# A two-layer hybrid encoder on one core: the modulation products on four 32-column tiles of TensorE, moved from the projections into the attention, and projection weights fetched three ahead

## The chip, the cores and the metric

One Trainium2 chip, of which the kernel uses one core. A core has five engines that run in parallel, each in the order of its own instruction stream: TensorE (PE, with its weight loads shown as PEld), VectorE (DVE), ScalarE (ACT), GpSimd (POOL) and SyncE (SP), which only issues DMAs here. The metric is the device time of one execution in microseconds (us).

## What is computed

The reference runs 1024 tokens of width 1024 through two layers. Each sub-layer is RMSNorm, a modulation `h * (1 + scale) + shift`, the sub-layer itself, and a gated residual add. Six vectors per layer (shift1, scale1, gate1, shift2, scale2, gate2) come from one condition vector:

```python
cond = jax.nn.silu(c)
shift1, scale1, gate1, shift2, scale2, gate2 = jnp.split(cond @ ada_w[i] + ada_b[i], 6, axis=-1)
h = modulate(rmsnorm(x, norm_mix_w[i]), shift1, scale1)
y = even_mixer(h, ...)      # layer 0: S5 state space | stick-breaking attention, one input projection
x = x + gate1[:, None, :] * y
h = modulate(rmsnorm(x, norm_ffn_w[i]), shift2, scale2)
x = x + gate2[:, None, :] * hierarchical_moe(h, ...)
```

So each of the 12 vectors ("names" below) is a product of a vector of 1024 with a 1024x1024 float32 matrix of 4 MiB. Layer 1 has other mixers; the change does not touch them.

## The kernel before

Everything that the change touches lies in layer 0, in `even` (L1979), ahead of the mixture of experts. Its work runs in these stages:

- **Prologue.** `norm_S` (L189) normalizes and transposes the tokens. The first 512 tokens are kept unmodulated until scale1 and shift1 of layer 0 are there (L2024), then `modulate` (L217) makes them, split into a high and a low part (`hTh`, `hTl`, by `split`, L136).
- **Projections.** Eight weights of 1 MiB (`wl`, L2040) are split by ACT and DVE into `wh` and `wl` (`wsplit`, L228), and TensorE multiplies them with the tokens by three matmuls for each product (`mm3`, L237): 768 matmuls of 128x512 in all. Weights come through `wload` (L74) into buffers of a ring (`ring`, L61); there are two rings of two 1 MiB buffers, and `pick` chooses one: ring 0 for the projection weights, one weight ahead, ring 1 for the modulation matrices.
- **S5 and attention.** Four S5 groups (`s5_quad`, L462) and eight query tiles of stick-breaking attention (`stick`, L283) are written in turn (L2087), and share DVE. A stick goes by key blocks: scores (L297, tile `ps_b`), two sigmoids on ACT (`keep`, `sw`), a mask on POOL, a scan on DVE (L313, tile `sP`), a product on POOL (L315), transposes (L106, `ps_a`), an eviction on ACT (L322), and the products with v (L326, `ps_d`), 288 of them in all. S5 uses the PSUM tag `e` (two banks), which the modulation products share.
- **GLU**, with the last sticks beside it (`glu`, tiles `gyh`, `gwh`), and the modulation of layer 1's shift2 and gate2.
- **Output rows.** `out_rows` makes two token tiles in float32 (L681), then the rest by `mm3` (first L240 of `ps_e<-wh,yh`).

The modulation products are made by `ada` (L142). For a name it loads four blocks of 1 MiB, each 128 partitions x 8 x 256. Most blocks go to DVE: one multiplication and seven multiply-adds of 128x256 (L160, L167) into `adacc`, whose 128 partitions TensorE then adds with a vector of ones (L179). One block of scale1 goes to TensorE directly (L177). Ten names are made before the GLU: scale1 and shift1 in the prologue, the other eight beside the projections, spread by the table `(0, 1, 1, 2, 2, 2, 0, 0)`.

The code is recorded in the order of the program, and a scheduler then sets the order of each engine's stream; so the place of an instruction is read below from the built program's order. A float32 matmul stands as two records in the trace (L326 has 288 matmuls in the code and 576 records); a transpose stands as one.

Of the kernel before, what the change touches and what calls it, by code (L numbers as in the profile page):

```python
# [9 lines left out]
FT = mybir.dt.float32  # L10
FR = mybir.dt.float32r
BF = mybir.dt.bfloat16
I32 = mybir.dt.int32
# [23 lines left out]
class Core:  # L37
# [42 lines left out]
    def consts(self):  # L80
        nc, c = self.nc, self.const
        ji = c.tile([128, 128], I32, name="ji")
        nc.gpsimd.iota(ji, pattern=[[1, 128]], base=0, channel_multiplier=-1)
        self.ident = c.tile([128, 128], FT, name="ident")
        nc.vector.tensor_scalar(self.ident, ji, 0.0, None, op0=OP.is_equal)
        self.ustrict = c.tile([128, 128], BF, name="ustrict")
        nc.vector.tensor_scalar(self.ustrict, ji, 0.0, None, op0=OP.is_gt)
        self.ones_b = c.tile([128, 128], BF, name="ones_b")
# [12 lines left out]
        nc.scalar.activation(self.cs, cr, AF.Silu)  # L101
        self.mod_d = self.dram.tile([2, 6, D], FT, name="mod_d")
# [39 lines left out]
    def ada(self, i, names, pool, tag, on_pe=((),), pool_eng=False):  # L142
# [4 lines left out]
        for m, nm in enumerate(names):  # L147
# [5 lines left out]
            for h in range(4):  # L153
                w = self.wload(aw[i, :, j * D + h * 256:j * D + (h + 1) * 256], 8)
                if h in on_pe[m % len(on_pe)]:
                    parts.append(w)
                    continue
                acc = pool.tile([128, 256], FT, name="adacc", bufs=4)
                eng = nc.gpsimd if pool_eng else nc.vector
                eng.tensor_scalar(acc, w[:, 0, :], self.cs[:, 0:1], None, op0=OP.mult)  # L160
                for k in range(1, KD):
                    wk, ck = w[:, k, :], self.cs[:, k:k + 1]
                    if pool_eng:
                        eng.tensor_scalar(wk, wk, ck, None, op0=OP.mult)
                        eng.tensor_tensor(acc, acc, wk, op=OP.add)
                    else:
# [4 lines left out]
            for h, x in enumerate(parts):  # L171
                for q in range(2):
                    qs = slice(q * 128, (q + 1) * 128)
                    p = pc[:, 2 * h + q:2 * h + q + 1]
                    if h in on_pe[m % len(on_pe)]:
# [1803 lines left out]
    def even(self, x_src):  # L1979
# [9 lines left out]
        with self.banks("pse", b=4, a=1, d=1, e=2):  # L1989
# [16 lines left out]
            with tc.tile_pool(name="hT", bufs=1, side="right") as hp, tc.tile_pool(name="wsp", bufs=1, side="right") as wp:  # L2006
# [178 lines left out]
```

## Time and profile before

| | us |
|---|---|
| median of 3 runs | 3071.89 (3069.78 to 3077.01) |
| profiled execution | 3069.93 |
| its span, first to last instruction | 3068.1 |
| of it, until the first projection matmul | 60.4 |
| projections | 223.8 |
| last projection matmul to the first sigmoid of the attention | 22.9 |
| S5 and attention, until the GLU | 240.9 |
| GLU | 92.6 |
| until the output rows by `mm3` | 57.9 |
| the rest: output rows, experts, layer 1 | 2369.6 |

Busy times are sums over one engine; a busy share is an average over stages with different limits. "Idle before" an instruction is time in which its engine stood, with what ended it. The granted clock of TensorE is given as a share of full speed; it has two levels, 2.4 and 1.2 GHz, so 0.94 over a stretch means that 12% of it ran at half speed.

### The profile page before, as it was taken

The numbers are of one execution on the slowest core, as the hardware profiler recorded it, in microseconds if no ns is written. First come the engines' busy times: TensorE is split into PE (matmuls) and PEld (weight loads), VectorE is DVE, ScalarE is ACT, GpSimd is POOL, SyncE is SP. The second block draws the span as 40 slices with busy tenths as digits, with TensorE's granted clock in tenths as the row PEclk, the third lists the DMA queues.
The fourth block names the chain that finished last, engine by engine and source line by source line (L and its number), as shares of the span: only waits on it lengthen the run. The fifth ranks groups of instructions, "written<-read, shape, count | busy, mean of one in ns | idle before, by whom it ended". The sixth has DMA issues, their size and how long they took to land. (4 is left out here: it accounts for less than half of the span.)

```text
span 3068.1 us, 39923 instructions
## 1 busy us (share of the span) xinstructions
PE 2656.4 (87%) x14357; PEld 1854.7 (60%) x14357; DVE 1792.6 (58%) x3211; ACT 1120.7 (37%) x1777; POOL 831.2 (27%) x1157
## 2 busy tenths in 40 slices
PE   4987688989699999995799999999978799998991
PEld 4776466647444466662677777777877444566660
DVE  7546999655633477664734555646547434556664
ACT  4311456432232345552433323323233223345451
POOL 5260755324211031101301533354105111111101
PEclk9998689989799999997898978886988799999996
DMA  8746220223588899997745322244443689999995
GB/s 279 178 124 198 63 59 15 90 68 105 211 338 324 351 368 407 376 389 256 260 138 176 110 77 78 67 121 103 107 125 119 242 348 365 369 362 396 388 385 239
DMA packets 345018, 672.82 MB, mean 219 GB/s; under 512 B 118591, under 2 KB 259935, under 8 KB 293104
## 3 DMA queue, kind: packets, MB, share of 16 engines
q1 hardware_dynamic: 272960, 611.23, 54.7%
q10 hardware_dynamic: 56752, 25.41, 3.0%
q0 software_dynamic: 15104, 33.58, 3.0%
q8 instruction: 115, 1.88, 0.3%
q14 instruction: 87, 0.71, 0.1%
HBM read 611.31 MB, written 79.79 MB: 225 GB/s over the span
## 5 line engine op out<-in xcount | busy, mean ns | idle before, releaser
L139 DVE TENSOR_TENSOR wlo<-w,whi 128x1024 fp32r<-128x1024 f32 x384 | 451.4, 1220 | 114.0 <-ACT whi L138 112.3
L138 ACT ACTIVATE whi<-w 128x1024 fp32r<-128x1024 f32 x384 | 390.5, 1054 | 237.1 <-PE ps_g L839 69.9
L240 PE MATMUL ps_b<-hTh,wh 128*128 128x512 f32 x608 | 259.3, 428 | 28.2 <-ACT cc L1382 12.5
L241 PE MATMUL ps_b<-hTl,wh 128*128 128x512 f32 x608 | 255.2, 420 | 0.0
L242 PE MATMUL ps_b<-hTh,wl 128*128 128x512 f32 x608 | 254.8, 419 | 0.0
L788 POOL DMA_INDIRECT xg<-h_d,tok x56 | 80.6, 1440 | 641.6 <-PE ps_t L106 617.1
L847 DVE TENSOR_TENSOR hs<-hs,ps_u 128x512 f32<-128x512 f32 x48 | 32.9, 685 | 263.3 <-PE ps_u L917 212.4
L794 POOL DMA_INDIRECT ye_d<-y,tab x48 | 71.9, 1497 | 421.8 <-DVE y L856 328.4
L167 DVE SCALAR_TENSOR_TENSOR adacc<-w,cs,adacc 128x256 f32<-128x256 f32 x329 | 161.1, 507 | 5.2
L139 DVE TENSOR_TENSOR wl<-w,wh 128x1024 fp32r<-128x1024 f32 x84 | 104.0, 1253 | 97.3 <-ACT wh L138 88.1
L240 PEld LDWEIGHTS ps_b<-hTh,wh 128*128 128x128 f32 x608 | 124.8, 206 | 55.9 <-ACT cc L1382 13.3
L846 ACT ACTIVATE hs<-ps_g 128x512 f32<-128x512 f32 x48 | 28.7, 598 | 325.0 <-PE ps_g L917 244.8
L313 DVE TENSOR_TENSOR_SCAN sP<-keep,sP,sbz 128x256 f32<-128x256 f32 (+1 forms) x160 | 132.9, 874 | 21.7 <-POOL keep L307 10.5
L917 PE MATMUL ps_g<-w,xh 128*64 128x512 f32 x512 | 143.5, 598 | 0.0
L133 POOL TENSOR_TENSOR rs<-rm,nhalf 128x1 f32<-128x1 f32 (+2 forms) x56 | 49.9, 892 | 344.9 <-DVE rm L131 293.2
L138 ACT ACTIVATE wh<-w 128x1024 fp32r<-128x1024 f32 x84 | 86.3, 1053 | 150.5 <-PE ps_b L241 132.4
L241 PEld LDWEIGHTS ps_b<-hTl,wh 128*128 128x128 f32 x608 | 124.7, 205 | 27.2 <-DVE hTl L139 0.3
L242 PEld LDWEIGHTS ps_b<-hTh,wl 128*128 128x128 f32 x608 | 123.9, 204 | 28.3 <-issue 0.4
L917 PE MATMUL ps_u<-w,xh 128*64 128x512 f32 x512 | 137.6, 595 | 0.0
L315 POOL TENSOR_TENSOR sw<-sw,sP 128x512 f32<-128x512 f32 (+1 forms) x80 | 101.1, 1265 | 132.6 <-DVE sP L313 57.3
L926 PE MATMUL ps_y<-w,hh 128*64 128x512 f32 x512 | 122.0, 598 | 2.2 <-ACT hh L921 2.2
L1699 POOL TENSOR_TENSOR T<-N,X 128x60 f32<-128x60 f32 (+24 forms) x248 | 87.1, 351 | 125.2 <-DMA N<-n_d 93.3
(709 smaller groups left out, 6177.9 us busy)
## 6 DMA issues: line engine op xcount, KB each, us to landing
w<-in_moe_w_gate_dram SPq DMA_DIRECT2D x128, 1024.0 KB, 14.7
w<-in_moe_w_up_dram SPq DMA_DIRECT2D x128, 1024.0 KB, 14.8
w<-in_moe_w_down_dram SPq DMA_DIRECT2D x128, 1024.0 KB, 13.4
w<-in_ada_w_dram SPq DMA_DIRECT2D x48, 1024.0 KB, 5.8
w<-in_odd_w_in_dram SPq DMA_DIRECT2D x26, 1024.0 KB, 5.7
cy<-ye_d SPq DMA_DIRECT2D x16, 1024.0 KB, 10.8
cx<-xm_d SPq DMA_DIRECT2D x29, 512.0 KB, 7.5
w<-in_even_w_in_dram SPq DMA_DIRECT2D x8, 1024.0 KB, 8.5
```

The source lines that it names most:

```text
L138: self.nc.scalar.activation(hi, x, AF.Copy)
L139: self.nc.vector.tensor_tensor(lo, x, hi.bitcast(FT), op=OP.subtract)
L167: eng.scalar_tensor_tensor(acc, wk, ck, acc, op0=OP.mult, op1=OP.add)
L240: nc.tensor.matmul(p, a[0], b[0], start=first, stop=False)
L241: nc.tensor.matmul(p, a[0], b[1], start=False, stop=False)
L242: nc.tensor.matmul(p, a[1], b[0], start=False, stop=last)
L313: v.tensor_tensor_scan(P[:, r, 0:n][:, ::-1], keep[:, r, 0:n][:, ::-1], zero.to_broadcast([128, n]), P[:, r, n:n + 1], op0=OP.mult, op1=OP ...
L315: g.tensor_tensor(w[:, :, 0:n], w[:, :, 0:n], P[:, :, 1:n + 1], op=OP.mult)
L788: nc.gpsimd.indirect_dma_start(out=xg, out_offset=None, in_=h_d[:], in_offset=bass.IndirectOffsetOnAxis(ap=tokc, axis=0), bounds_check=T - ...
L917: nc.tensor.matmul(ps[z][r], x[:, 4 * h + k, r], w[z][h][:, k, :], start=(h == 0 and k == 0), stop=(h == 1 and k == 3))
L926: nc.tensor.matmul(py[n][r], ht[:, f, r], w[2][f // 2][:, f % 2, two[n]], start=(f == 0), stop=(f == 3))
L1699: g.tensor_tensor(o, N[:, 0:j, j:j + 1].to_broadcast([128, j, w]), X[:, j:j + 1, c:8].to_broadcast([128, j, w]), op=OP.mult)
```

## The change

1. `ada` makes every product on TensorE. A stationary operand `csz` (128x8x32) holds the condition in column 0 of 32 and zeros in the others. For each block, matmul k (k = 0 to 7) multiplies 128x256 of the matrix with column k of the condition on the column tile `32 * (k % 4)` of TensorE, so the four tiles each add two of the eight; ACT copies the PSUM bank of 128x512 to `adacc`, and TensorE adds its partitions with ones, as before.
2. The eight names are taken out of the projections and put between the sticks, one for each stick.
3. The projections use both rings: three weights are loaded ahead, and the next is asked for three ahead.
4. `ji` shares its memory with `ident`; the order of two constants turns.

```diff
+        self.csz = c.tile([128, KD, 32], FT, name="csz")
+        nc.vector.memset(self.csz, 0.0)
+        nc.vector.tensor_copy(self.csz[:, :, 0:1], self.cs[:, :, None])
...
-            for h in range(4):
-                w = self.wload(aw[i, :, j * D + h * 256:j * D + (h + 1) * 256], 8)
-                if h in on_pe[m % len(on_pe)]:
-                    parts.append(w)
-                    continue
-                acc = pool.tile([128, 256], FT, name="adacc", bufs=4)
-                eng = nc.gpsimd if pool_eng else nc.vector
-                eng.tensor_scalar(acc, w[:, 0, :], self.cs[:, 0:1], None, op0=OP.mult)
-                for k in range(1, KD):
...
-                        eng.scalar_tensor_tensor(acc, wk, ck, acc, op0=OP.mult, op1=OP.add)
+            for h2 in range(2):
+                pa = self.psum(tag)
+                for h in (2 * h2, 2 * h2 + 1):
+                    w = self.wload(aw[i, :, j * D + h * 256:j * D + (h + 1) * 256], 8)
+                    for k in range(KD):
+                        q = 32 * (k % 4)
+                        nc.tensor.matmul(pa[q:q + 32, h % 2 * 256:h % 2 * 256 + 256], self.csz[:, k, :], w[:, k, :],
+                                         start=(k < 4), stop=(k >= 4), tile_position=(0, q))
+                acc = pool.tile([128, 512], FT, name="adacc", bufs=2)
+                nc.scalar.activation(acc, pa, AF.Copy)
                 parts.append(acc)
             yield
             pc = self.psum(tag)
...
+            for n in range(KD):
+                nc.tensor.matmul(pc[:, n:n + 1], parts[n // 4][:, n % 4 * 128:n % 4 * 128 + 128], self.ones_f[:, 0:1], start=True, stop=True)
...
-                    list(self.ada(0, ["scale1", "shift1"], ap, "e", ((2,), ())))
+                    list(self.ada(0, ["scale1", "shift1"], ap, "e"))
...
-                pick(0)
-                w = {0: wl(0)}
-                wv, late = [], []
+                w = {n: wl(n) for n in range(3)}
+                wv = []
                 for n in range(8):
-                    if n < 7:
-                        pick(0)
-                        w[n + 1] = wl(n + 1)
+                    if n + 3 < 8:
+                        w[n + 3] = wl(n + 3)
...
-                    pick(1)
-                    for _ in range((0, 1, 1, 2, 2, 2, 0, 0)[n]):
-                        for x in late:
-                            list(x)
-                        i, nm = todo.pop(0)
-                        late = [self.ada(i, [nm], ap, "e")]
-                        next(late[0])
...
                     self.s5_quad(Q, prm, u_d, g_d, s5)
                     for i in si:
+                        for x in late:
+                            list(x)
+                        late = [self.ada(j, [nm], ap, "e") for j, nm in todo[:1]]
+                        todo = todo[1:]
+                        for x in late:
+                            next(x)
                         stick(i)
```

How the streams move is read from the order of the built programs. First DVE at the end of the prologue, around the vector shift1 of layer 0. Before:

```order
L167 SCALAR_TENSOR_TENSOR adacc<-w,cs,adacc 128x256 x3
L131 TENSOR_SCALAR rm_452<-ss 128x1
L167 SCALAR_TENSOR_TENSOR adacc<-w,cs,adacc 128x256
L160 TENSOR_SCALAR adacc<-w,cs 128x256
L167 SCALAR_TENSOR_TENSOR adacc<-w,cs,adacc 128x256 x5
L160 TENSOR_SCALAR adacc<-w,cs 128x256
L167 SCALAR_TENSOR_TENSOR adacc<-w,cs,adacc 128x256 x8
L139 TENSOR_TENSOR wl<-w,wh 128x1024
L167 SCALAR_TENSOR_TENSOR adacc<-w,cs,adacc 128x256
L139 TENSOR_TENSOR wl<-w,wh 128x1024
L180 TENSOR_TENSOR shift_0_282<-ps_e,adac 128x8
```

And in the changed program:

```order
L135 TENSOR_SCALAR rm_393<-ss 128x1
L135 TENSOR_SCALAR rm_443<-ss 128x1
L135 TENSOR_SCALAR rm_453<-ss 128x1
L173 TENSOR_TENSOR shift_0_281<-ps_e,adac 128x8
L143 TENSOR_TENSOR wl<-w,wh 128x1024 x4
L143 TENSOR_TENSOR hTl<-hm,hTh 128x2x256 x8
```

The multiply-adds are gone from DVE, and all four halves of the first two projection weights (`wl`) stand ahead of the tokens' low parts (`hTl`).

Second, SP's queue from the last modulation loads of the prologue on. Before:

```order
L2013 DMA xt<-in_x_dram 128x1024
L77 DMA w<-in_ada_w_dram 128x8x256 x2
L77 DMA w<-in_even_w_in_dram 128x8x256 x2
L77 DMA w<-in_ada_w_dram 128x8x256 x2
L77 DMA w<-in_even_w_in_dram 128x8x256 x2
L77 DMA w<-in_ada_w_dram 128x8x256 x4
L262 DMA u_d<-ut 1024x1x64 x2
L77 DMA w<-in_even_w_in_dram 128x8x256
```

And in the changed program:

```order
L2006 DMA xt<-in_x_dram 128x1024
L77 DMA w<-in_even_w_in_dram 128x8x256 x6
L255 DMA u_d<-ut 1024x1x64 x2
L77 DMA w<-in_even_w_in_dram 128x4x512
L255 DMA u_d<-ut 1024x1x64 x5
L77 DMA w<-in_even_w_in_dram 128x4x512
L255 DMA u_d<-ut 1024x1x64
L77 DMA w<-in_ada_w_dram 128x8x256 x4
L540 DMA u_1844<-u_d 32x4x128 x8
L576 DMA g_d<-yo 32x4x128 x4
```

The projection weights stand in one run, and only four modulation loads (the first name's) stand ahead of the S5 inputs (`u<-u_d`).

Third, TensorE behind the first S5 group (its last products are `ps_e<-hi,CA`). Before:

```order
L578 MATMUL ps_e<-hr,CA_2186 128x128
L578 MATMUL ps_e<-hi,CA_2187 128x128
L106 MATMUL ps_e<-ident,cl 128x128
L326 MATMUL ps_d<-swT,v 64x128 x4
L106 MATMUL ps_a<-ident,sw 128x128 x4
L297 MATMUL ps_b<-kT,qT 128x256 x2
L106 MATMUL ps_e<-ident,cl 128x128
```

And in the changed program, where `ps_e<-w,csz` are the tile matmuls, eight for a block:

```order
L571 MATMUL ps_e<-hr,CA_1716 128x128
L571 MATMUL ps_e<-hi,CA_1717 128x128
L164 MATMUL ps_e<-w,csz 32x256 x16
L319 MATMUL ps_d<-swT,v 64x128 x2
L110 MATMUL ps_a<-ident,sw 128x128 x2
L164 MATMUL ps_e<-w,csz 32x256 x16
L172 MATMUL ps_e<-ones_f,adacc 128x1 x4
L110 MATMUL ps_a<-ident,sw 128x128 x2
L290 MATMUL ps_b<-kT,qT 128x256 x2
L172 MATMUL ps_e<-ones_f,adacc 128x1 x4
```

The first moved name stands here as two runs of 16. Over the whole stream: until the last S5 product TensorE has 180 of the 288 products with v before and 176 now, with the tile matmuls of four moved names; from there to the GLU 14 before and 60 now, with four names (twelve of their loads stand in SP's queue in that piece); beside the GLU 54 and 52, with the last two names now; behind it 40 before and none now.

## Rows read from the trace of the kernel before

**Rows 1.** The page: the span, and busy time of each engine over the whole span.

```profile
span 3068.1 us, 39923 instructions
PE 2656.4 (87%) x14357; PEld 1854.7 (60%) x14357; DVE 1792.6 (58%) x3211; ACT 1120.7 (37%) x1777; POOL 831.2 (27%) x1157
```

**Rows 2.** Busy time by stretch: start and end, length, busy time and count of PE, PEld, DVE, ACT and POOL, the granted clock, DMA share and GB/s. The stretches are the prologue, the projections, the step to the attention, S5 and attention to the last S5 product, from there to the GLU, the GLU, and the first output rows.

```profile
0.00:60.40 60.40, 23.17 (x101) 20.52 (x101) 43.60 (x91) 24.73 (x41) 36.23 (x27) 1.00 0.96 314
60.40:284.20 223.80, 206.42 (x907) 170.05 (x907) 130.52 (x354) 47.04 (x59) 64.92 (x179) 0.94 0.64 170
284.20:307.10 22.90, 5.40 (x23) 3.53 (x21) 10.67 (x32) 2.31 (x2) 5.38 (x7) 0.62 0.63 115
307.10:537.80 230.70, 184.55 (x1250) 131.29 (x1250) 226.09 (x389) 121.77 (x261) 146.48 (x136) 0.82 0.17 46
537.80:548.00 10.20, 7.38 (x64) 4.50 (x63) 5.84 (x12) 8.96 (x17) 3.01 (x6) 1.00 0.43 144
548.00:640.60 92.60, 83.20 (x458) 58.56 (x458) 60.97 (x100) 33.60 (x61) 25.43 (x24) 0.93 0.26 80
640.60:698.50 57.90, 49.48 (x212) 26.15 (x211) 25.68 (x40) 23.16 (x40) 15.84 (x25) 0.85 0.20 61
```

**Rows 3.** The prologue in order of time: start, duration, engine, line, operation, and in brackets the idle time of the engine before it and what ended that.

```profile
14.21 1.03 DVE L160 TENSOR_SCALAR adacc<-w,cs 128x256 f32<-128x256 f32 x1 [1.61 <-DMA w<-in_ada_w_dram]
...
44.47 3.75 DVE L167 SCALAR_TENSOR_TENSOR adacc<-w,cs,adacc 128x256 f32<-128x256 f32 x8
...
50.86 0.17 DVE L180 TENSOR_TENSOR shift<-ps_e,adac 128x8 f32<-128x8 f32 x1
...
54.34 0.69 DVE L139 TENSOR_TENSOR hTl<-hm,hTh 128x512 fp32r<-128x512 f32 x1 [0.55 <-ACT hTh L138]
...
60.40 1.22 PE L240 MATMUL ps_b<-hTh,wh 128*128 128x512 f32 x2 [9.58 <-ACT hTh L138]
```

**Rows 4.** Busy time by stretch for the first 40 us; the last two columns are the DMA share and GB/s.

```profile
0.00:20.00 20.00, 4.20 (x16) 3.00 (x16) 6.86 (x20) 8.26 (x14) 12.57 (x13) 1.00 0.95 292
20.00:40.00 20.00, 16.14 (x73) 14.94 (x74) 17.66 (x39) 6.65 (x12) 12.00 (x7) 1.00 1.07 372
```

**Rows 5.** Groups of instructions by line between 0 and 700 us: busy time, mean ns of one, and the idle time before them.

```profile
L167 DVE SCALAR_TENSOR_TENSOR adacc<-w,cs,adacc 128x256 f32<-128x256 f32 x329 | 161.1, 507 | 5.2
...
L322 ACT ACTIVATE swT<-ps_a 128x512 f32<-128x512 f32 (+1 forms) x80 | 44.6, 558 | 124.6 <-PE ps_a L106 99.9 <-issue 7.1 <-DVE bb L338 6.5
...
L160 DVE TENSOR_SCALAR adacc<-w,cs 128x256 f32<-128x256 f32 x47 | 21.4, 455 | 71.8 <-DMA w<-in_ada_w_dram 71.0 <-PE ps_e L179 0.7
```

**Rows 6.** Busy time by stretch of the instructions on the tile `adacc` alone: PE, PEld, DVE.

```profile
60.40:284.20 223.80, 15.54 (x112) 17.08 (x112) 98.85 (x222) 0.94 0.64 170
...
307.10:548.00 240.90, 1.03 (x5) 0.93 (x4) 21.62 (x38) 0.83 0.18 50
548.00:698.50 150.50, 3.95 (x32) 3.88 (x32) 14.00 (x32) 0.90 0.24 73
```

**Rows 7.** The same for the tile `sP` of the sticks: DVE, POOL.

```profile
307.10:548.00 240.90, 111.52 (x170) 73.53 (x58) 0.83 0.18 50
```

**Rows 8.** TensorE at the end of the projections, in order of time: the first and the last of 20 matmuls of 128x512 that follow each other.

```profile
279.88 0.40 PE L241 MATMUL ps_b<-wl,hTh 128*128 128x512 f32 x1
...
284.19 0.39 PE L242 MATMUL ps_b<-wh,hTl 128*128 128x512 f32 x1
```

**Rows 9.** Five waits of TensorE inside the projections, in order of time.

```profile
95.85 0.79 PE L240 MATMUL ps_b<-hTh,wh 128*128 128x512 f32 x1 [2.27 <-ACT ut L261]
...
112.73 0.79 PE L240 MATMUL ps_b<-hTh,wh 128*128 128x512 f32 x1 [3.58 <-ACT c L383]
...
196.62 0.61 PE L179 MATMUL ps_e<-ones_f,adacc 128*128 128x1 f32 x4 [1.98 <-DVE adacc L167]
...
211.81 1.01 PE L179 MATMUL ps_e<-ones_f,adacc 128*128 128x1 f32 x4 [4.24 <-DVE adacc L167]
...
228.78 1.01 PE L179 MATMUL ps_e<-ones_f,adacc 128*128 128x1 f32 x4 [2.83 <-DVE adacc L167]
```

**Rows 10.** The step to the attention in order of time; ACTq and SPq are the engines' queues, where the time is that of issuing.

```profile
286.34 3.89 SPq L77 DMA_DIRECT2D w<-in_ada_w_dram  x2
...
287.63 8.57 ACTq L473 DMA_DIRECT2D bl<-in_s_b_im_dram  x1
...
305.81 1.28 ACT L300 ACT_TABLE_LOAD   x1 [17.78 <-DMA cl<-in_s_c_im_dram]
```

**Rows 11.** TensorE in order of time: matmuls on the whole array (L681, stationary 128x128), on two 64-column tiles in turn (L326 and L917, stationary 128x64), and the whole array behind tiles (L106).

```profile
362.27 0.66 PE L326 MATMUL ps_d<-swT,v 128*64 128x128 f32 x8
362.85 0.44 PE L106 MATMUL ps_a<-ident,sw 128*128 128x128 f32 x2
...
640.65 3.68 PE L681 MATMUL ps_e<-w,gl 128*128 128x512 f32 x8
...
850.90 2.80 PE L917 MATMUL ps_g<-w,xh 128*64 128x512 f32 x12
```

**Rows 12.** Behind the GLU and inside it, in order of time: a wait of DVE for a modulation load, the last product with v, and the first output row by `mm3`.

```profile
611.46 0.35 DVE L160 TENSOR_SCALAR adacc<-w,cs 128x256 f32<-128x256 f32 x1 [5.90 <-DMA w<-in_ada_w_dram]
...
672.31 0.69 PE L326 MATMUL ps_d<-swT,v 128*64 128x128 f32 x4 [0.53 <-ACT swT L322]
...
698.49 0.79 PE L240 MATMUL ps_e<-wh,yh 128*128 128x512 f32 x1
```

More of the change, by code (lines that the diff above doesn't have):

```diff
@@ L81, in consts @@
         nc, c = self.nc, self.const
-        ji = c.tile([128, 128], I32, name="ji")
+        self.ident = c.tile([128, 128], FT, name="ident")
+        ji = self.ident[:].bitcast(I32)
         nc.gpsimd.iota(ji, pattern=[[1, 128]], base=0, channel_multiplier=-1)
-        self.ident = c.tile([128, 128], FT, name="ident")
-        nc.vector.tensor_scalar(self.ident, ji, 0.0, None, op0=OP.is_equal)
         self.ustrict = c.tile([128, 128], BF, name="ustrict")
         nc.vector.tensor_scalar(self.ustrict, ji, 0.0, None, op0=OP.is_gt)
+        nc.vector.tensor_scalar(self.ident, ji, 0.0, None, op0=OP.is_equal)
         self.ones_b = c.tile([128, 128], BF, name="ones_b")
@@ L139, in split, with ada @@
         self.nc.vector.tensor_tensor(lo, x, hi.bitcast(FT), op=OP.subtract)
-    def ada(self, i, names, pool, tag, on_pe=((),), pool_eng=False):
+    def ada(self, i, names, pool, tag):
         nc, a, c = self.nc, self.a, self.const
@@ L146, in ada @@
         aw, ab = a["ada_w"], a["ada_b"]
-        for m, nm in enumerate(names):
+        for nm in names:
             j = order.index(nm)
@@ L170, in ada @@
             pc = self.psum(tag)
[L171 to L175, printed above, removed]
-                        for k in range(KD):
-                            nc.tensor.matmul(p, x[:, k, qs], self.cs[:, k:k + 1], start=(k == 0), stop=(k == KD - 1))
-                    else:
-                        nc.tensor.matmul(p, x[:, qs], self.ones_f[:, 0:1], start=True, stop=True)
+            for n in range(KD):
+                nc.tensor.matmul(pc[:, n:n + 1], parts[n // 4][:, n % 4 * 128:n % 4 * 128 + 128], self.ones_f[:, 0:1], start=True, stop=True)
             nc.vector.tensor_tensor(o, pc[:, 0:KD], b, op=OP.add)
@@ L2061, in even @@
                         self.s5_phasors(prm, s5e, wp)
-                    pick(1)
-                    for _ in range((0, 1, 1, 2, 2, 2, 0, 0)[n]):
-                        for x in late:
-                            list(x)
-                        i, nm = todo.pop(0)
-                        late = [self.ada(i, [nm], ap, "e")]
-                        next(late[0])
-                for x in late:
-                    list(x)
-                self.rings = both
             sb = pool(left, "sbp", "left")
@@ L2089, in even @@
                 self.s5_blocks(prm, s5)
+                late = []
                 for Q, si in enumerate(((1, 2), (3,), (4,), (5, 6, 7, 0))):
@@ L2092, in even @@
                     for i in si:
+                        for x in late:
[4 more added lines that the diff above has]
+                            next(x)
                         stick(i)
+                for x in late:
+                    list(x)
             phasors.close()
```

5 lines of the change are left out of this document (removed).

## The prediction

> **What bounds the kernel now.** The profiled execution took 3069.93 us for a span of 3068.1 [rows 1], 2 us under the median of 3071.89; the sum below is made against 3069.93. No engine bounds the whole span, so I read it by stages first [rows 2], and look in each for the engine that is nearly full. The change lies ahead of 698.5 us; what follows should shift as a whole.
>
> In the prologue VectorE bounds: from its first block at 14.21 us it works almost without a pause until shift1 is there at 50.86, and the first projection matmul at 60.40 had waited 9.58 us for tokens that need shift1 [rows 3]. In the projections TensorE is busy for 206.4 of 223.8 us, at a clock of 0.94 [rows 2]; its larger waits are few, and three of five are for `adacc` [rows 9]. From 307.1 to 537.8 VectorE bounds: 226.1 of 230.7 us, 98%, where TensorE has 184.6 at a clock of 0.82 [rows 2]. Beside the GLU TensorE is the fuller one again (83.2 of 92.6). From 640.6 to 698.5 two work lists stand one behind the other: sticks are left until 672.31, and the output rows of the token tile they end, then `mm3` at 698.49 [rows 12].
>
> **What a name costs.** On VectorE a block is one multiplication and seven multiply-adds, 0.455 + 7 x 0.507 = 4.0 us [rows 5], so a name 16 us. Of this work 98.9 us lie in the projections, 21.6 in the attention and 14.0 behind it [rows 6].
>
> On TensorE a name is now 4 x 8 matmuls of 256 columns, 64 records. No row shows four 32-column tiles, so I bound them. On the whole array eight records of 512 columns take 3.68 us, 0.46 each; on two 64-column tiles twelve take 2.80, 0.23 each [rows 11]. Two tiles thus share the time of one. A record of 256 columns alone would be 0.23, a name 14.7 us if tiles do not overlap, 7.4 if two do, 3.7 if four do. I take 3.7: the pair of tiles shows whole overlap with different data on each, and consecutive matmuls of a block go to different tiles; 14.7 stays as the end. The sums with ones are moved, not added. ACT gets two copies of 128x512 for a name, 1.1 us at 0.558 each [rows 5]; beside 121.8 busy of 230.7 us [rows 2] I cost them at nothing; without that cover they would be 9 us for the eight moved names.
>
> A rule of the skill gives another price. The Trainium skill, "TensorE: Matmul & The Clock Gate", section "Measured speedup vs the span model", has 2.38 times for three column tiles. In proportion four would give 3.2 times, an estimate from that page: a name of 4.6 us instead of 3.7, and a sum some 4 us later. No run here shows three or four tiles.
>
> **Prologue: -6.** The eight modulation loads and eight token tiles are 12.6 MB. At 292 and 372 GB/s, 13.3 MB had come by 40 us [rows 4], so the last modulation load lands near 38.4. With the last block's matmuls, one copy, the sum and hand-overs shift1 is there at about 41 instead of 50.86. But the two first projection weights land behind it in the same queue, the second near 44; ACT splits it for 2 us, and VectorE's order now has all `wl` ahead of `hTl`, so the first `hTl` starts near 48.4 instead of 54.34 [rows 3]. From there to the first projection matmul took 6.1 us: 54.4 instead of 60.4. The ends are -10 (the split does not hold the tokens back) and -2.
>
> **Projections: -36.** The work is 768 matmuls at 0.227 us (19 steps from 279.88 to 284.19, [rows 8]), 174.3 us. Against 223.8, three things go. TensorE's 15.5 us on `adacc` [rows 6], of which I count 13, since the last record of each group overlaps the matmul behind. The three waits for `adacc`, 9.05 us [rows 9]. And clock: at 0.94 the stretch lost 6%, 13.4 us; the five waits are 14.9 us, and in proportion the three lost 8.1. That is 30. The other two waits are for ACT (5.85 us and 5.3 of clock); one is for `c`, which comes out of a VectorE chain among the multiply-adds, so I count about half, 6. The ends are -30 and -44 (to 180, all waits gone). Weights three ahead add nothing of their own: none of the five waits was for a weight. The queue pays for the order: the projection loads stand in one run, and modulation loads no longer pass them.
>
> **Step to the attention: -6.** ACT's first sigmoid waited 17.78 us for its small S5 loads, whose issue stood 8.57 us, with two modulation loads in flight from 286.34 [rows 10]. Those are 2.1 MB, 5.6 us at 372 GB/s [rows 4]; now the first name's four loads stand ahead of this and find their buffers free during the v projection. Ends 0 and -12.
>
> **S5 and attention to the last S5 product: -20.** The sticks in it are about the same (180 and 176 products with v). VectorE loses 21.6 us of 226.1 [rows 2, 6]; four names are 15 us more for TensorE, which would have 200 of 210. I take 20 and not more, since the second name's loads wait in a ring of four for the first name's matmuls: four loads, 11 us, while TensorE's order has few sticks to do. Ends -25 and 0.
>
> **From there to the GLU: +38.** Now 60 products with v stand here instead of 14, with four names. The last 40 took 640.65 to 672.31, 0.8 us each [rows 11, 12], so 48 us against 10.2 [rows 2]. VectorE alone would need 111.5/194 = 0.57 each, 34 us [rows 7]; twelve loads of 2.8 us also 34. Ends +26 and +50.
>
> **GLU: +2.** 52 products with v instead of 54. Two names on TensorE add 7.4 us; VectorE's wait of 5.90 us for a load [rows 12] goes with its 14 us of multiply-adds. Ends -5 and +10.
>
> **Output rows: -27.** No sticks are left, so 64 records of 0.46 us, 29.4, stand between the GLU and `mm3`, and the weight splits lie beside them; with a little for the router's sums, 31 instead of 57.9. Ends -20 and -30.
>
> Sum: -6 - 36 - 6 - 20 + 38 + 2 - 27 = -55, so 3069.93 - 55 = **3015 us**. A second rule speaks against the change: by the Trainium skill, "TensorEngine Tiling (Array Packing)", section "Key Properties", a change of the tiling mode drains TensorE. The trace agrees: eight records on tiles start 0.055 apart (half of 0.109 alone), yet the next whole-array record comes 0.58 us after the first [rows 11], some 0.14 late. The tile matmuls stand in about 28 runs outside the prologue, 56 switches, 8 us; only those beside the GLU lie on a full TensorE, so by the rule the sum is 2 us later.
>
> **Rivals.**
> *The tiles do not overlap, and TensorE becomes the bound (slower).* A name is then 14.7 us. In the prologue a block's matmuls (3.7) outlast its load (2.8), +3. In the attention 44 us more meet a slack of some 14, +30. Between S5 and GLU the 60 products at 0.65 us of TensorE are 39 (their three lines have 125 us of its 191.9 there for 194) and four names 59, so 98 for 48; I take +45, as the clock would rise. The GLU gets +22. Together +100: 3115 us. It decides from about 9.5 us for a name on, an overlap under 1.5. For it: no row shows four streams at once. Against it: the rows of two.
> *Tiles overlap in pairs, or loads come late.* At 7.4 us, +21 between S5 and GLU, +7 in the GLU, +2 elsewhere: 3045. Late loads reach the same: SP's queue has the GLU's weights behind the eighth name's loads, each block of which waits for a buffer.
> *VectorE's multiply-adds were only filler.* Then projections and attention do not shorten, and -6 - 6 + 38 + 2 - 27 = +1: 3071, no change. For it: the scheduler puts such work where it sees room. Against: [rows 3, 9], and 98% busy.
> *All goes well.* Projections -44, the step -12, attention -25, sticks between S5 and GLU near their VectorE time, +26, GLU 0, the rest as above: -88, 2982.
>
> **How the numbers follow.** Chances: forecast 0.56 (2990 to 3040), all well 0.15, pairs or late loads 0.15, filler 0.06, no overlap 0.08. The first three are faster by over 0.2% (6 us, about what a measurement of this kernel can tell from no change): 0.86; same 0.06; slower 0.08. The range, 2978 to 3058, takes in the forecast with the ends of its terms, the case in which all goes well, and pairs or late loads; it leaves out filler and no overlap, and some of the edges, where layer 1's order also turns a little.
>
> **What would show it.** Right: tile records of 256 columns four within 0.23 us; shift1 near 41 and the first projection matmul near 54 us; projections near 188 us with no wait over 2 us for `adacc`; the last S5 product near 473 us, the GLU at 521, `mm3` at 643. Wrong: tile records 0.2 us apart on TensorE; waits of TensorE for modulation loads in the attention; a GLU that waits for its weights.

## The result: slower by 0.7%, and where the time went

The changed kernel took **3094.28 us** (median of 5 runs, 3091.33 to 3100.22) against 3072.09 before: a ratio of **1.0073** (95% interval 1.0057 to 1.0089). The forecast was 3015. The profiled execution's span is 3091.0 us, 22.9 more than before.

Busy time by stretch in the profile after, with the columns and the stages of [rows 2]:

```profile
0.00:54.90 54.90, 23.69 (x201) 14.44 (x201) 10.29 (x29) 26.90 (x46) 34.89 (x27) 0.83 1.03 344
54.90:242.00 187.10, 182.36 (x794) 149.45 (x795) 37.78 (x124) 46.30 (x58) 57.78 (x178) 0.98 0.17 47
242.00:248.10 6.10, 2.04 (x11) 0.74 (x9) 2.16 (x13) 2.32 (x3) 5.63 (x8) 1.00 0.49 109
248.10:506.80 258.70, 203.80 (x1531) 142.85 (x1532) 209.12 (x346) 124.15 (x265) 129.41 (x134) 0.84 0.29 81
506.80:579.40 72.60, 58.09 (x587) 36.20 (x586) 36.71 (x58) 35.77 (x65) 23.09 (x24) 0.91 0.97 250
579.40:666.20 86.80, 82.96 (x541) 58.35 (x541) 30.71 (x49) 27.36 (x55) 14.23 (x21) 0.94 0.44 136
666.20:699.50 33.30, 30.18 (x87) 14.40 (x87) 16.08 (x24) 11.02 (x13) 5.33 (x10) 1.00 0.45 96
```

| stage | before | after | moved | forecast |
|---|---|---|---|---|
| prologue | 60.4 | 54.9 | -5.5 | -6 |
| projections | 223.8 | 187.1 | -36.7 | -36 |
| step to the attention | 22.9 | 6.1 | -16.8 | -6 |
| S5 and attention, to the last S5 product | 230.7 | 258.7 | +28.0 | -20 |
| from there to the GLU | 10.2 | 72.6 | +62.4 | +38 |
| GLU | 92.6 | 86.8 | -5.8 | +2 |
| output rows until `mm3` | 57.9 | 33.3 | -24.6 | -27 |
| the rest | 2369.6 | 2391.5 | +21.9 | 0 |

Up to the first sigmoid of the attention the change is 59 us ahead, more than forecast. In the 451.4 us from there to `mm3` (391.4 before) all of it is lost, and a further 22 us go behind `mm3`, in code that the change does not touch. The rest by stretch, before and then after: experts of layer 0, mixers of layer 1, experts of layer 1 (the end, 76.5 and 77.0 us, is left out).

```profile
698.50:1405.10 706.60, 659.47 (x2970) 413.03 (x2970) 393.81 (x663) 276.07 (x335) 128.85 (x89) 0.97 0.82 325
1405.10:2412.90 1007.80, 869.16 (x5915) 690.77 (x5911) 551.80 (x1130) 331.96 (x662) 321.86 (x606) 0.83 0.42 130
2412.90:2991.60 578.70, 556.36 (x2425) 332.41 (x2426) 309.53 (x369) 240.72 (x283) 72.49 (x51) 0.99 0.91 365
```

```profile
699.50:1408.10 708.60, 659.41 (x2973) 410.49 (x2972) 394.08 (x664) 277.49 (x336) 132.29 (x90) 0.97 0.82 324
1408.10:2425.20 1017.10, 861.44 (x5913) 684.93 (x5909) 551.83 (x1130) 331.50 (x662) 317.19 (x606) 0.83 0.42 129
2425.20:3014.00 588.80, 562.79 (x2424) 332.99 (x2425) 311.15 (x369) 241.91 (x283) 73.50 (x51) 0.99 0.91 359
```

The instructions are the same within a few records, and TensorE's busy times within 1.2%; the mixers take 9.3 us longer and the experts of layer 1 10.1.

**The tiles do overlap.** TensorE behind the first S5 group of the changed kernel, in order of time (the place of the third piece of order above):

```profile
308.23 1.93 PE L164 MATMUL ps_e<-w,csz 128*32 128x256 f32 x32
310.09 0.44 PE L319 MATMUL ps_d<-swT,v 128*64 128x128 f32 x4
310.46 0.44 PE L110 MATMUL ps_a<-ident,sw 128*128 128x128 f32 x2
310.82 1.93 PE L164 MATMUL ps_e<-w,csz 128*32 128x256 f32 x32
312.69 1.05 PE L172 MATMUL ps_e<-ones_f,adacc 128*128 128x1 f32 x8
...
314.58 1.05 PE L172 MATMUL ps_e<-ones_f,adacc 128*128 128x1 f32 x8
```

32 records in 1.93 us are 0.060 each with the last one's tail, at a granted clock of 1.00, where a record of 256 columns alone would be 0.23 by [rows 11], at the same clock: 3.8 times. My estimate from the Trainium skill's "TensorE: Matmul & The Clock Gate" ("Measured speedup vs the span model") was 3.2 times for four; the trace is better, and nothing hangs on it. But 64 records and 16 sums stand here in front of the next scores: over these 7.4 us TensorE does little for the sticks. What VectorE does then:

```profile
315.67 0.17 DVE L173 TENSOR_TENSOR adao<-ps_e,adac 128x8 f32<-128x8 f32 x1 [6.75 <-PE ps_e L172]
318.19 1.40 DVE L306 TENSOR_TENSOR_SCAN sP<-keep,sP,sbz 128x256 f32<-128x256 f32 x2 [2.35 <-POOL keep L300]
...
325.43 2.31 DVE L306 TENSOR_TENSOR_SCAN sP<-keep,sP,sbz 128x256 f32<-128x256 f32 x2 [5.64 <-ACT keep L293]
```

It stands for 6.75 us until the name's sum is there, and later for 5.64 us for a sigmoid. That second wait begins at ACT, whose stream holds small transfers:

```profile
319.56 0.38 ACTq L180 DMA_DIRECT2D mod_d<-adao  x1
323.56 0.38 ACTq L115 DMA_DIRECT2D adac<-in_ada_b_dram  x1
324.03 0.38 ACT L315 ACTIVATE swT<-ps_a 128x256 f32<-128x256 f32 x1 [6.92 <-DMA w<-in_ada_w_dram]
```

By the profile ACT's stream, with a 4 KB load and the evictions behind it, goes on here only when a 1 MiB modulation load has landed. So there were two theories for the attention: **A**, the loads (1 MiB loads keep small transfers, and with them ACT and VectorE, waiting), and **B**, TensorE's stream (a name's work is added, not hidden). For the rest, **H**: the order into which the scheduler turned layer 1, and **I**: something that layer 0 leaves behind. "The stretch" below is that from the first sigmoid to `mm3`, "the attention" its part up to the last S5 product.

### The profile page after: what moved, and what is told of

Read it like the earlier page. It is cut to its first block, busy times and chain, and to the rows that moved or that the text cites. A ratio compares the mean times of both kernels' runs of the same rounds, so it can differ in the third digit from the quotient of the medians.

```text
span 3091.0 us, 41083 instructions
## 1 busy us (share of the span) xinstructions
PE 2678.6 (87%) x15097; PEld 1848.7 (60%) x15097; DVE 1634.0 (53%) x2837; ACT 1135.1 (37%) x1801; POOL 804.9 (26%) x1157
## 5 line engine op out<-in xcount | busy, mean ns | idle before, releaser
L781 POOL DMA_INDIRECT xg<-h_d,tok x56 | 90.8, 1622 | 646.2 <-PE ps_t L110 620.2
L787 POOL DMA_INDIRECT ye_d<-y,tab x48 | 64.5, 1344 | 426.5 <-DVE y L849 343.8
L840 DVE TENSOR_TENSOR hs<-hs,ps_u 128x512 f32<-128x512 f32 x48 | 32.9, 686 | 259.4 <-PE ps_u L910 209.1
L308 POOL TENSOR_TENSOR sw<-sw,sP 128x512 f32<-128x512 f32 (+1 forms) x80 | 92.3, 1154 | 113.5 <-DVE sP L306 38.4
L110 PE MATMUL ps_t<-ident,xg 128*128 128x128 f32 (+1 forms) x448 | 75.5, 304 | 45.8 <-DMA w<-in_moe_w_down_dram 17.3
## 6 DMA issues: line engine op xcount, KB each, us to landing
w<-in_moe_w_down_dram SPq DMA_DIRECT2D x128, 1024.0 KB, 12.6
```

Of the source, the lines that this page charges most:

```text
L110: self.nc.tensor.transpose(out, in_, self.ident[:n, :n])
L308: g.tensor_tensor(w[:, :, 0:n], w[:, :, 0:n], P[:, :, 1:n + 1], op=OP.mult)
L781: nc.gpsimd.indirect_dma_start(out=xg, out_offset=None, in_=h_d[:], in_offset=bass.IndirectOffsetOnAxis(ap=tokc, axis=0), bounds_check=T - ...
```

## The experiments

Ratios are to runs of the kernel before on the same chip, where its median was 3077 to 3088 us; the stretches of e1 to e12 are compared with 391.4 us before and 451.4 after. Each stretch is read from one profile. The order of before gave 396.2 on another chip (e7) and that of the change 456.2 (e11), so differences of 5 us say nothing.

**e1: no loads.** `w[:, k, :]` of the eight moved names is a constant.

```diff
-                    w = self.wload(aw[i, :, ...], 8)
+                    w = self.wload(aw[i, :, ...], 8) if load else None
+                        wk = w[:, k, :] if load else self.csz[:].rearrange("p k c -> p (k c)")
```

> The eight moved names multiply a constant tile of 128x256 instead of their matrix: their 32 loads of 1 MiB are left out (so the vectors have other values), and the tile matmuls, copies and sums stay. In the changed kernel the attention lasted 258.7 us to the last S5 product (forecast 211) and 72.6 from there to the GLU (forecast 48). Theory A, the loads: ACT and SP issue small transfers (biases, S5 constants, u) that come in behind 1 MiB loads, ACT's stream stops at them and VectorE starves; without the loads the attention lasts 215 to 228 us and the GLU begins 40 to 50 us behind it. Rival B, TensorE's stream: the tile matmuls and sums stand ahead of the scores of the sticks and hold them back, 5 us a name at half clock; then the attention stays above 250 us. Rival C, the clock or the order alone: also above 250.

```profile
248.70:496.30 247.60, 197.01 (x1508) 140.44 (x1509) 204.82 (x344) 121.39 (x261) 133.40 (x132) 0.85 0.11 17
496.30:550.60 54.30, 47.81 (x481) 30.69 (x480) 23.65 (x40) 26.71 (x47) 11.88 (x15) 0.87 0.22 47
```

The attention fell by 11 us only, to just under the 250 of rivals B and C, and the piece behind it by 18. The GLU and the output rows behind them took back 22, so the stretch fell from 451.4 to 443.9. Theory A carries 7.5 us of 60.

**e2: the small transfers leave ACT.**

```diff
-            b = self.col(pool, ab[...], "adac", KD)
+            b = self.col(pool, ab[...], "adac", KD, nc.sync)
...
-                nc.scalar.dma_start(self.mod_d[i, j]..., o)
+                nc.sync.dma_start(self.mod_d[i, j]..., o)
```

> The biases, norm weights and stores of the modulation vectors (5 + 2 + 5 transfers of 4 KB in the attention) are issued by SP instead of ACT; nothing else is edited. Theory A (ACT's stream stops at these): the two stops of ACT seen in the changed kernel, 6.9 us at 324 and 9.6 us at 403.5, go, and the attention gets 12 to 20 us shorter (239 to 247). Rival D (what is late is S5's own input u and its constants, whoever issues the biases): the attention stays within 5 us of 258.7, and new stops stand at the S5 constants. Rival B: no change either.

The attention lasted 254.3 us (4.4 less), the stretch 458.9 (7.5 more); ratio to before 1.0073 (1.0053 to 1.0092), as the change. But ACT went on stopping, for S5's input and for a bias (waited for: us in total, times, longest):

```profile
ACT swT L315 <- DMA u<-u_d: 10.4, 2, 8.4
ACT swT L315 <- DMA adac<-in_ada_b_dram: 8.3, 1, 8.3
```

So e2 does not tell what such stops cost; it shows what rival D had named, new stops and an attention within 5 us. Theory A fell with e1, where the 1 MiB loads are gone.

**e3 and e4: tiles and place apart.** e3 has the tiles and the place of before, e4 VectorE and the place of the change.

```diff
 # e3, against the change
+                    pick(1)
+                    for _ in range((0, 1, 1, 2, 2, 2, 0, 0)[n]):
+                        ...
+                        late = [self.ada(i, [nm], ap, "e")]
```

> The products stay on four column tiles, but the eight names go back beside the projections with the table and the one weight ahead of the kernel before. TensorE's sum there: 182 us + 8 names x 3.4 (64 records 0.053 apart) + 7 sums x 1.9 = 223, so the projections last 225 to 232 us. Theory A: no 1 MiB load is left in the attention, which then lasts about 205 to 215 us (before 230.7, of them 21.6 of multiply-adds), the output rows by mm3 begin near 655 to 670. Rival B: the tile matmuls hold the projections back by more, over 240 us. Its layer 1 has the order of the changed kernel to within 4 of 6884 matmuls: if the 22 us lost behind the output rows come from that order, the rest lasts 2388 to 2394 us here too; if they come from what layer 0 left behind (loads, clock, time), it lasts near the 2369.6 of before.

```profile
54.10:337.70 283.60, 248.34 (x1418) 184.13 (x1419) 38.96 (x133) 55.51 (x74) 55.82 (x178) 0.89 0.59 150
343.60:724.80 381.20, 322.95 (x2102) 217.24 (x2102) 286.80 (x463) 188.24 (x382) 179.38 (x189) 0.90 0.20 56
```

The stretch without the eight names is 381.2 us. Its attention, 210.4 us, is what theory A had put, but B would have the same, as no moved name lies in it. The projections came out 52 us over the upper end of my range: TensorE is busy 66 us more than in the change, and stands 27.6 us in four waits for loads, one of them below. (That a load comes late because a ring of two buffers is free only when TensorE has done the block before is argued, not shown.)

```profile
221.94 1.51 PE L164 MATMUL ps_e<-w,csz 128*32 128x256 f32 x12 [8.35 <-DMA w<-in_ada_w_dram]
```

The total ratio is 1.011 (1.0091 to 1.013). The rest lasted 2393.7 us (2391.5 in the change), with the change's order of layer 1 and another layer 0 ahead of it: for H.

```diff
 # e4, against the kernel before
-                w = {0: wl(0)}
+                w = {n: wl(n) for n in range(3)}
...
                     for i in si:
+                        for x in late:
+                            list(x)
+                        late = [self.ada(j, [nm], ap, "e") for j, nm in todo[:1]]
+                        ...
                         stick(i)
```

> The kernel before with its products by VectorE, but the eight names moved to the sticks and projection weights three ahead, as in the change: the place without the tiles. Theory A: 1 MiB loads and small transfers collide as in the changed kernel, and VectorE has 16 us more for a name, so with four names the attention lasts 290 to 320 us, and the total is 3130 to 3190. Rival B (the tiles do the harm): the attention lasts no more than 258 us.

```profile
252.30:747.20 494.90, 361.64 (x2101) 252.69 (x2101) 407.19 (x764) 187.54 (x377) 189.16 (x189) 0.80 0.41 101
```

The attention to the last S5 product lasted 252.8 us, less than I expected; the piece from there to the GLU took 102.4, the whole stretch 494.9, with VectorE busy for 407. Ratio 1.0187 (1.0167 to 1.0206). The place costs more with VectorE than with the tiles. VectorE's work on `adacc` in this stretch (PE, PEld, DVE):

```profile
252.30:747.20 494.90, 24.42 (x160) 23.77 (x160) 140.75 (x288) 0.80 0.41 101
```

That is 105.1 us more than the 35.6 of before [rows 6], and the stretch is 103.5 us longer: added here, VectorE's work for a name counts about whole too, its load included.

**e5 and e6: TensorE's work for a name, none and more.**

```diff
 # e5, ahead of a name's loads
+            if not make:
+                nc.vector.memset(o, 0.5)
+                ...
+                continue
 # e6
-                    for k in range(KD):
+                    for k in [k for _ in range(times) for k in range(KD)]:
```

> The changed kernel with the eight moved names left out: no loads, tile matmuls, copies or sums, their vectors are a constant (so what the experts do behind it is another thing and is not read). Measured is the stretch from the first sigmoid of the attention to the first output row by mm3: 391.4 us before, 451.4 in the change, 443.9 in e1 (without loads), 381.2 in e3 (names in the projections). Theory B, new form: no single engine bounds the stretch, the sticks go round through all engines, so TensorE's work for a name (6.3 us busy: 50 us more in the stretch for eight) is added whole; then 376 to 388 us here. Rival G: the sticks and S5 are slower in this kernel for another reason (S5's inputs and weights that come earlier, the two rings), and it stays over 425.

```profile
289.40:674.00 384.60, 331.11 (x2099) 221.96 (x2100) 294.17 (x464) 188.99 (x382) 175.52 (x188) 0.87 0.18 55
```

> The changed kernel with every tile matmul of the eight moved names done twice (the second time over the first, the vectors are the same): 512 records more, 27 us at full clock and 55 at half. Theory B (TensorE's work is added whole): the stretch from the first sigmoid to mm3 grows from 451.4 to 472 to 500 us. Theory A (loads and small transfers hold it): it stays within 10 us of 451.

```profile
247.70:731.10 483.40, 402.47 (x3253) 269.81 (x3253) 290.27 (x476) 198.40 (x398) 175.61 (x188) 0.90 0.41 112
```

Both as theory B has it. For comparison the stretch before, and then after:

```profile
307.10:698.50 391.40, 324.61 (x1979) 220.50 (x1978) 318.58 (x539) 187.49 (x378) 190.77 (x189) 0.86 0.20 59
```

```profile
248.10:699.50 451.40, 375.03 (x2740) 251.79 (x2741) 292.62 (x476) 198.30 (x397) 172.06 (x189) 0.88 0.44 120
```

With the names on TensorE, its busy time and the stretch go together: 331 and 384.6 (e5), 375 and 451.4 (after), 402 and 483.4 (e6), with 53 to 81 us in which TensorE stands. Before, with VectorE's 35.6 us of adds, the stretch is longer than e5's although TensorE has less. 512 records more cost 32 us, 4.0 us for a name's 64; the name as a whole, without loads, 7.4 (443.9 less 384.6, by eight), with them 8.4. Of the 67 us between e5 and the change, 44 are TensorE's busy time and 7.5 go with the loads; the other 15 (hand-overs, ACT's copies, small transfers, the order) are not taken apart. The names also share S5's two PSUM banks, and no run gives them banks of their own. In the trace of the change the sums wait 2.8 us in all for ACT's copies out of such a bank (the last number below), so this rival looks small, but it is not tested:

```profile
L172 PE MATMUL ps_e<-ones_f,adacc 128*128 128x1 f32 x160 | 20.1, 249 | 2.8 <-ACT adacc L167 2.8
```

The ratio of e6 is 1.0166 (1.0147 to 1.0184).

**e7 and e8: parts of the change put into the kernel before.**

```diff
 # e7, against the kernel before
+        ji = self.ident[:].bitcast(I32)
...
+        self.csz = c.tile([128, KD, 32], FT, name="csz")
+        nc.vector.memset(self.csz, 0.0)
```

> The kernel before with only part 4 and the constant csz of the change (ident shares its memory with ji, csz is made and not used): apart from three instructions on constants every engine has the order of before. Theory H (the 22 us lost behind the output rows are the order of layer 1, which a scheduler turned): the rest from mm3 on is that of before, 2370 us, or up to 2382 where this chip is slower throughout; total as before within 0.2%. Rival I (memory places or the constants themselves): the rest is 2388 or more.

Ratio 1.0006 (0.9988 to 1.0023); the rest 2371 us. The constants, and what part 4 does to memory places, are out.

```diff
 # e8, against the kernel before
-                    list(self.ada(0, ["scale1", "shift1"], ap, "e", ((2,), ())))
+                    list(self.ada_t(0, ["scale1", "shift1"], ap, "e"))
-                    for _ in range((0, 1, 1, 2, 2, 2, 0, 0)[n]):
+                    for _ in range((1, 1, 2, 2, 2, 0, 0, 0)[n]):
```

> The kernel before with four column tiles for scale1 and shift1 alone, and the other names by VectorE beside the projections one step earlier each (table 1, 1, 2, 2, 2, 0, 0, 0 for 0, 1, 1, 2, 2, 2, 0, 0). Prologue 55 us instead of 60.4 as in the change; step to the attention 6 to 12 us instead of 22.9, since no modulation load is left in flight there; projections 220 to 230 instead of 223.8; attention as before. So mm3 begins 12 to 25 us earlier than before, near 673 to 687. By theory H the rest is a matter of its own order: 2370 to 2400, so the total is between 40 us less and 10 more than before.

The prologue took 55.3 us, as expected; the projections 239.7 (229.4 in e7 on the same chip) and the step 17.1 missed it. `mm3` came at 700.1, 5.6 us ahead of e7; with 2388.4 us of rest the ratio is 1.0045 (1.0033 to 1.0058). The edits cost the projections 10 us; which of them is open (beside the two shown, `adacc` is kept here in two buffers of 128x512 instead of four of 128x256).

**e9 and e10: the same products without sums.** Each block of a name gets its own column tile and is added up in PSUM:

```diff
+        for k in range(KD):
+            for h in range(4):
+                nc.tensor.matmul(pa[32 * h:32 * h + 32, :], self.csz[:, k, :], w[h][:, k, :],
+                                 start=(k == 0), stop=(k == KD - 1), tile_position=(0, 32 * h))
+        nc.vector.tensor_tensor(b, pa, b, op=OP.add)
...
+        nc.sync.dma_start(row(dst), acc[::32, 0:256])
```

> The changed kernel with the eight moved names made without sums: each of the four blocks of a name has a column tile of its own, the eight products are added in PSUM (k outside, block inside), and the result stands in four rows, so the 16 records with ones and the two copies of 128x512 on ACT are gone, and bias and result go as four rows of 1 KB; loads are asked for one stick ahead of the tile matmuls. Theory B (TensorE's work for a name is added whole to the stretch of 384.6 us that e5 has without names): the tile matmuls alone were 36 us busy for eight names, the sums 16; so the stretch from the first sigmoid to mm3 is 420 to 437 us instead of 451.4. Rival A (loads and their waits): 444 or more, since the loads are the same. What speaks for longer: in its order the GLU stands behind the last stick.

```profile
247.10:681.20 434.10, 362.96 (x2613) 239.27 (x2613) 298.33 (x476) 188.65 (x381) 178.14 (x194) 0.88 0.41 125
```

```diff
 # e10; turn() ends the name under way and begins the next
+                turn()
                 for Q, si in enumerate(((1, 2), (3,), (4,), (5, 6, 7, 0))):
+                    if Q:
+                        turn()
                     self.s5_quad(Q, prm, u_d, g_d, s5)
                     for i in si:
+                        turn()
                         stick(i)
```

> As e9, with the names begun earlier: the first name's loads stand ahead of the first S5 group, and a name also at each further S5 group, so that seven of eight names stand ahead of the last S5 product and the GLU has sticks beside it. Theory B: the same TensorE work as e9, so the stretch is within 10 us of it, 415 to 437 us, wherever the names stand. mm3 then begins at 664 to 686 us, 12 to 35 earlier than before. With 2390 to 2400 behind it (the order of layer 1 in every changed program so far, against 2371 in before and e7) the total is 3055 to 3085 where before is 3072 to 3087.

434.1 and 431.2 us: 12 to 15 us less of TensorE, 17 to 20 less of stretch, wherever the names stand. (Copies, small transfers on ACT's queue and late loads went with the sums, so not all of it need be the sums.) `mm3` began at 681.2 and 680.0, 17 and 18 us ahead of before. But the rest took 2403.7 and 2409.0, more than I expected, so the ratios are 0.9979 (0.9961 to 0.9996) and 1.0026 (1.0014 to 1.0037).

**e11 and e12: another order of layer 1.** Small loads that nothing uses turn the scheduler's order:

```diff
+    xx = k.const.tile([128, KD], FT, name="xx")
+    for _ in range(2):                                   # 7 in e12, ahead of the experts of layer 0
+        nc.sync.dma_start(xx, a["c"][0].rearrange("(k p) -> p k", p=128))
     if ODD:
```

> The changed kernel with two small loads (4 KB each, of the condition, into a tile that nothing uses) added on SP's queue, where they land in the prologue. Their only effect is on the scheduler: in layer 0 up to the experts the order of TensorE is that of the changed kernel, and behind it that of the kernel before to within 12 of 6655 matmuls. Theory H (the 22 us lost behind the output rows are the order of layer 1): the output rows by mm3 begin as in the change, at 695 to 708 us, and the rest lasts 2369 to 2382 us instead of 2391; the total is within 0.4% of before. Rival I (what layer 0 leaves behind, memory places, the tiles as such): the rest stays at 2388 to 2400 and the total at 0.7% above before.

```profile
252.00:708.20 456.20, 375.58 (x2741) 251.32 (x2741) 293.26 (x476) 198.63 (x397) 172.76 (x189) 0.88 0.46 119
708.20:1416.60 708.40, 659.51 (x2971) 410.79 (x2971) 393.06 (x663) 277.63 (x336) 130.77 (x89) 0.97 0.82 325
1416.60:2432.10 1015.50, 869.54 (x5912) 691.85 (x5908) 550.64 (x1129) 331.43 (x662) 318.95 (x606) 0.83 0.43 130
2432.10:3008.30 576.20, 555.80 (x2424) 332.62 (x2425) 309.42 (x369) 240.84 (x283) 70.07 (x51) 0.99 0.91 365
```

The stretch, 456.2 us, is that of the change within 5, the rest 2377.6 us instead of 2391.5: the experts are back at 576, the mixers stay 8 us over before. Ratio 1.0039 (1.0023 to 1.0055), although the small loads cost the prologue 4 us. H carries 14 of the 22 us; the 8 in the mixers are open.

> As e9, with the first name's loads ahead of the first S5 group and one name for each stick, and with seven such small loads on SP's queue, which again give layer 1 the order of the kernel before to within 12 of 6655 matmuls. Theories B and H together: the stretch from the first sigmoid to mm3 425 to 440 us as in e9 and e10, mm3 at 676 to 690 us (the small loads may cost the prologue 0 to 6 us), the rest 2369 to 2382, so the total is 10 to 28 us under that of before (ratio 0.991 to 0.997). Rival I: the rest stays at 2390 to 2410 as in every changed order so far, and the total is within 0.3% of before or above it.

```profile
255.10:678.80 423.70, 354.80 (x2611) 235.71 (x2612) 298.89 (x477) 187.81 (x380) 179.43 (x194) 0.91 0.43 128
```

The stretch came out just below my range, `mm3` at 678.8, the rest 2381.2, where the mixers took 1018.5, as in the change, and the experts of layer 1 579.3, as before. So it is the experts' time that the order gives back, in e11 and here. **3059.01 us against 3077.13 on this chip, a ratio of 0.9939 (0.992 to 0.9958): faster than both kernels.** How firmly such an order holds under the next edit is another matter; the same rows in the order of e9 are 0.2% ahead of before, in that of e10 0.3% behind.

## Why the prediction was wrong

**What held.** The overlap of four tiles; the prologue (-5.5 for -6), the projections (-36.7 for -36, `adacc` and its waits gone: TensorE is busy 24.1 us less and stands 12.6 less), the output rows (-24.6 for -27: no stick is left there). The step to the attention was right in kind, with the wait of [rows 10] gone, and lay outside its ends (-16.8, ends 0 and -12), as did the GLU (-5.8, ends -5 and +10).

**The step that failed** is in "S5 and attention: -20": four names "are 15 us more for TensorE, which would have 200 of 210". I read VectorE's 98% in [rows 2] as the bound, and so took the names on TensorE as hidden, at nothing. They are added whole, and more. The stretch is 384.6 us without the eight moved names (e5) and 451.4 with them; 44 of these 67 us are TensorE's own busy time, and the same tile matmuls done twice add 32.0 us of stretch for 27.4 us of busy time (e6). A stick goes round all engines in order, so a name's records and sums in TensorE's stream delay the next scores, and VectorE then stands, as in the rows at 315 us. In the change VectorE, which was to be the bound, is busy for 81% of the attention (209.1 of 258.7 us).

**The other half of that step**, that VectorE's 21.6 us of multiply-adds come back as time, is neither shown nor refuted. The attention of e5, with no name in it:

```profile
289.40:497.90 208.50, 168.63 (x1149) 121.94 (x1149) 202.24 (x328) 110.21 (x239) 126.32 (x125) 0.84 0.09 20
```

It lasted 208.5 us where I forecast 211, and VectorE is again busy for 97%. But less of the sticks lies in it, by the tile `sP` (DVE, POOL) before and then in e5:

```profile
307.10:537.80 230.70, 107.05 (x162) 71.24 (x55) 0.82 0.17 46
```

```profile
289.40:497.90 208.50, 95.69 (x144) 58.43 (x48) 0.84 0.09 20
```

Over the whole stretch e5 is 6.8 us shorter than before (11.6 shorter than e7 on the same chip), with all of VectorE's 21.6 and 14.0 us [rows 6] gone and the two names of the GLU on TensorE instead. So some of the adds may have filled gaps, as the rival "only filler" said, to which I gave 0.06; how much is open. Adds put between the sticks were no filler: they cost 103.5 us for 105.1 in e4.

The stretch of my sum, 211 + 48 + 94.6 + 31 = 384.6 us, is that of e5: I had forecast a kernel without the moved names. That it agrees so closely is luck, as the pieces differ (208.5, 10.6, 97.4 and 68.1 in e5, where the sticks come later). The 67 us that lie between are eight names at 8.4.

**A sum that was not charged.** "The sums with ones are moved, not added": I took 13 us for them off the projections, and nothing came on in the attention. The two tiles' busy times there (ten names, two of them in the GLU) show it:

```profile
242.00:699.50 457.50, 46.21 (x640) 20.12 (x640) 0.00 (x0) 0.88 0.44 120
```

```profile
242.00:699.50 457.50, 20.06 (x160) 19.24 (x160) 11.99 (x20) 0.88 0.44 120
```

The first is `csz` (PE, PEld, DVE), the second `adacc` (PE, PEld, ACT): 4.6 and 2.0 us of TensorE for a name, where I had 3.7 and none. ACT's copies, which I cost at nothing, are 12.0 us; what they cost apart from the sums is open. In e9 the sums and copies are gone, and the stretch is 17 us shorter.

**From there to the GLU** (+62.4 for +38) failed by the same step: four names stand in it, and I priced the sticks alone. Its DMA share of 0.97 looks like a bound, but e1 without the moved loads is 18 us shorter there and only 7.5 in the stretch.

**"What follows should shift as a whole"** was not so: +21.9 us. Ahead of the result I had seen that layer 1's order turns a little, and priced it in the edges alone. With before's order back, 14 of the 22 come back (e11); the cause of the 8 in the mixers is open.

**The rivals.** The only case that was slower, "The tiles do not overlap", had 0.08 and 3115 us for TensorE as the bound; its premise was false and its place right, since even overlapped tiles are added to the stretch. "Only filler" would have left the projections as they were; they are 36.7 us shorter. My first theory after the result, the loads, fell too: 7.5 us.

## What to carry over

That one engine is busy for 98% of a stretch does not make room on the others: in a loop that goes round several engines, charge a new instruction on any of them at its full time (here 32.0 us of stretch for 27.4 us on TensorE, and 103.5 for 105.1 on VectorE), and time the loop without the new work as well, as e5 does, to see what it hides. Count a moved step whole at its new place: its sums, copies and small transfers too. Where a scheduler sets the order, an edit can turn code that it does not touch; compare the untouched part by itself before you explain the total.

## Seen of the hardware

Four 32-column tiles with float32 data overlap to 3.8 times one, at a granted clock of 1.00. The same records took longer elsewhere, first in the prologue, then in the attention:

```profile
39.72 1.93 PE L164 MATMUL ps_e<-w,csz 128*32 128x256 f32 x16
...
387.90 5.35 PE L164 MATMUL ps_e<-w,csz 128*32 128x256 f32 x64
```

The granted clock there is the third number from the end (of the tile `csz`: PE, PEld, DVE):

```profile
39.70:41.70 2.00, 1.93 (x16) 0.60 (x16) 0.00 (x0) 0.50 1.08 385
...
387.80:394.00 6.20, 5.35 (x64) 2.68 (x64) 0.00 (x0) 0.72 0.35 33
```

That is 0.121 us a record at 0.50, the level of 1.2 GHz, and 0.084 at 0.72, a mix of both levels; 0.060 divided by the clock is 0.120 and 0.083. So the clock accounts for it, and over the whole stretch a name cost 4.6 us and not 3.7.

ACT's longest stop in the attention was 9.55 us, by the profile until a 4 KB load had landed:

```profile
403.46 0.60 ACT L315 ACTIVATE swT<-ps_a 128x512 f32<-128x512 f32 x1 [9.55 <-DMA adan<-in_norm_mix_w_dram]
```

The 1 MiB loads do not explain that one. The next of them was issued at 398.80, and for the 4.9 us ahead of it the DMA engines were almost idle (share 0.04 below, in the columns of [rows 2]), against 1.09 in the stop of 6.92 us shown above:

```profile
316.90:324.00 7.10, 1.32 (x20) 0.43 (x8) 1.57 (x4) 0.21 (x1) 1.25 (x2) 0.96 1.09 368
393.90:398.80 4.90, 1.96 (x14) 1.22 (x13) 3.75 (x8) 0.01 (x1) 0.00 (x0) 0.97 0.04 0
```

What held it is open.

The 64 KB loads of S5's input took 10.9 us from issue to landing in the change, 2.2 before, and 2.6 in e1, without the moved loads:

```profile
u<-u_d SPq DMA_DIRECT2D x32, 64.0 KB, 10.9
```

```profile
u<-u_d SPq DMA_DIRECT2D x30, 64.0 KB, 2.2
```

```profile
u<-u_d SPq DMA_DIRECT2D x25, 64.0 KB, 2.6
```

Neither set the time here: e1 is 7.5 us shorter in the stretch.
